# Norms two blocks ahead, output chains in halves, and W_down sums left in PSUM: four edits to a hybrid decoder layer

## The chip, the cores and the metric

The kernel runs on one core of one Trainium2 chip. The metric is device time in microseconds (us). Three runs of the kernel before took 1760.06, 1757.07 and 1756.71 us, with a median of 1757.07. The engines are named as in the profile: PE (matmuls and transposes), PEld (its weight loads), DVE, ACT, POOL, and SP, which issues the DMAs.

## The reference

One decoder layer over 16 learned meta tokens and 1024 tokens, width 1024, all in float32:

```python
def rms_norm(x, g):
    x32 = x.astype(jnp.float32)
    y = x32 * lax.rsqrt(jnp.mean(x32 * x32, axis=-1, keepdims=True) + EPS)
    return (y * g.astype(jnp.float32)).astype(x.dtype)
...
        xn = rms_norm(h, mix_pre_g[l])
        proj = xn @ w_in[l]
...
        y_ssd = ssd_mixer(z, xbc, dt_raw, ssd_conv_w[l], ssd_conv_b[l], ssd_dt_bias[l],
                          ssd_a_log[l], ssd_d[l], ssd_norm_g[l])
        y_sb = rms_norm(stick_breaking_attention(q, k, v).reshape(Bsz, L, SB_WIDTH), sb_norm_g[l])
        mix = jnp.concatenate([y_ssd, y_sb], axis=-1) @ w_out[l]
        h = h + rms_norm(mix, mix_post_g[l])
        xn = rms_norm(h, ffn_pre_g[l])
        gu = xn @ w_up[l]
        g = causal_dwconv(gu[..., :D_FF], ffn_conv_w[l], ffn_conv_b[l])
        f = (jax.nn.gelu(g, approximate=True) * gu[..., D_FF:]) @ w_down[l]
        h = h + rms_norm(f, ffn_post_g[l])
```

`ssd_mixer` is a chunked state-space mixer with a convolution of four taps ahead of it. `stick_breaking_attention` takes, for each of 16 heads of 64, scores z = q.k/8, the logs of sigmoid(z) and of 1 - sigmoid(z), a running sum of the second over the keys behind each key, and the exponential of both together as the weight of v. Keys lie strictly before the query. D_FF is 2816, and the FFN's convolution has three taps.

## The kernel before

**Splits.** Every product is taken at nearly full float32 precision: an operand is split into a high part of the matmul format fp32r (`hi`, a copy on ACT) and a low part (`lo`, original minus high, on DVE or POOL), and three matmuls are summed: hi·hi, lo·hi, hi·lo. A split is thus one ACT copy and one subtraction per tile, and the subtraction's place (DVE or POOL) is chosen line by line.

**Stages in order of time.**

1. *Opening.* The tokens come in nine blocks: block 0 holds the 16 meta rows, blocks 1 to 8 hold 128 tokens each. For each block `load_x` issues the DMA on SP, `square` (L260, ACT) sums the squares, `root` (L190, POOL) makes the reciprocal root, `norm` (L270, DVE, tile xn in a ring of two) scales, and `turn_x` (L282) transposes the block with eight PE matmuls into xtp, copies the high part on ACT (L287) and subtracts the low part on DVE (L289), tile xs. The first projection, pj_dt (L220), reads the first 400 columns, that is blocks 0 to 3. The order on every engine is the order in which this code is written.
2. *SSD part*, then *attention* over eight head pairs p = 0 to 7. In each pair the queries run in eight blocks i. `block_weights` makes scores z (L754) on PE, kp and bt (L755, L756) on ACT, a scan of kp (L762) on DVE and the sum into bt (L764) and a border column cb (L765) on POOL. `block_turn` transposes bt on PE into tw (L776), ACT makes th of it (L778), and `block_mix` multiplies with v into av (L791). A block goes through these stages over three turns of the loop. Between them stand fill steps from the next pair's projections (`fill`, from pj_v and others), so that PE has work while DVE, POOL and ACT are busy. Only PE's order is written by hand here; the others follow the tile framework's priorities. `turn_edge` handles the keys that lie across block borders (edge L419 and L420 on DVE, vtc L422 on PE).
3. *Last pair.* Pair 7 has no next projections. Its fill is the SSD half of the output projection W_out: `ssd_half` makes, for each token block t, two chains mo of 24 matmuls (`out_steps`, L936), one per half of the 1024 output columns, and ACT scales the result into ma (L951). One chain runs per turn of the loop (`run(first, 1)`). The y blocks are split by `split_y` (L925 yh on ACT, L926 yl on POOL). The weights of W_out are woa. `halo_rows` (L905 to L911) multiplies the two y rows ahead of the first token, in four column groups of PE, 64 matmuls of 256 columns (the profile shows two records for each), and takes the result out with four ACT copies mh (L910) and four DMAs into halod. The accumulators mo and halo come from `psum_mm`, a ring of two PSUM banks named mm.
4. *Second half of W_out and the norms* (x2 transposes at L1116), `halo_block` for the two rows ahead of the tokens.
5. *FFN up* in seven Strassen–Winograd products (L1254), with the convolution and the gate (L1319, L1326); their results go to DRAM as fds and fda.
6. *W_down*, also seven products. `DOWN` lists them as (number, left factor, right factor); each has 11 steps, so 77 steps. `down_mm` (L1652) makes 12 matmuls a step, three for each of four row tiles t, into the banks dn. `split_step` (L1568 to L1583) splits both factors of the step three ahead: dh on ACT (L1581), dl on DVE, but on POOL for the right factor in the last 14 steps (`LATE`, L1582). The rings whi and wlo hold three steps. For product 6 it also makes the sum t2 (L1579). `W_SUMS` (L1586) says at which step the sums b11, b21, b12 of weight blocks are made on DVE. When a product is done, `evac2` (L1654 to L1669) adds the bank into up to three accumulators facc in SBUF, one tile per step through the list `todo`. `half_tail`, `close_tail` and `end_tail` (L1682 to L1707) make the last norm: a square on ACT (L1687), a product with the gain on DVE (L1688), the root on POOL (L1697, L1698), the residual on DVE (L1706) and the DMA out. For the upper half of the rows (h = 0) they run beside products 7 and 4, for the lower half at the end, where the last four steps are walked tile by tile.

Tile names carry buffer numbers, which the profile leaves out.

Of the kernel before, what the change touches and what calls it, by code (L numbers as in the profile page):

```python
# [51 lines left out]
def tile_layer(ctx: ExitStack, tc: tile.TileContext, x, meta, rows, parts,  # L52
# [80 lines left out]
    halod = [dr.tile([2, D], F32, name=f"halod{n}", tag=f"halod{n}") for n in range(2)]  # L133
# [92 lines left out]
    with tc.tile_pool(name="pre", bufs=3, side="right") as pre, \  # L226
# [134 lines left out]
    def qkv_steps(p, post):  # L361
# [67 lines left out]
        post += [lambda: turn_v(0), lambda: turn_v(1), turn_edge]  # L429
# [471 lines left out]
    def halo_rows(pool, half, y0, w, acc):  # L901
        for k in range(8):
            for s in range(2):
                for c in range(4):
                    mm(acc[32 * c:32 * c + 2, 0:256], y0[:, k, :], w[k][s][:, 256 * c:256 * c + 256].bitcast(F32),  # L905
                       start=k == 0 and s == 0, stop=k == 7 and s == 1)
        mh = pool.tile([P, 256], F32, tag="ma", name=f"mh{half}", bufs=1)
        for c in range(4):
            rows_ = slice(32 * c, 32 * c + 2)
            nc.scalar.activation(mh[rows_], acc[rows_, 0:256], AF.Copy)  # L910
            nc.sync.dma_start(out=halod[half][:, 256 * c:256 * c + 256], in_=mh[rows_])  # L911
# [7 lines left out]
    def split_y(pool, half, t, tags, yk=None):  # L919
# [6 lines left out]
        nc.gpsimd.tensor_tensor(yl, yk, yh.bitcast(F32), op=ALU.subtract)  # L926
# [15 lines left out]
    def ssd_half(w, ys):  # L942
        for t in range(1, NT + 1):
            y = ys.pop(0)
            if t < NT - 1:
                ys.append(split_y(wp, 0, t + 2, ("whi", "wlo", WB)))

# [6 lines left out]
            yield from out_steps(0, t, w, y, ev)  # L954
# [19 lines left out]
    for p in range(8):  # L974
        for i in range(NT):
# [8 lines left out]
            run(fill, 1 + (i < FILL[p]))  # L984
            run(block)
# [71 lines left out]
    for _ in first:  # L1057
        run(second, 2)
# [659 lines left out]
    for s in range(n2):  # L1718
# [33 lines left out]
        if s + 5 < n2:  # L1752
            fetch_a(s + 4)
# [90 lines left out]
```

## Time and profile before

| | |
|---|---|
| median of three runs | 1757.07 us |
| the profiled execution's own time | 1754.64 us |
| its span | 1752.8 us |
| mean granted PE clock | 0.994 |
| PE busy | 1711.4 us (98%), 11358 matmuls |
| DVE, ACT, POOL busy | 1127.2, 820.2, 890.3 us |
| DMA | 173.87 MB, mean 99 GB/s |

The rows of the profile read as follows. A row of the timeline has start and duration in us, the engine, the line of the kernel, the operation, output and inputs by tile name, the shapes and a count; in brackets stands how long the engine was idle before it and what it was waiting for. A count over one means that the operations of a row follow each other closely. The duration of a matmul is longer than the distance to the next one, because they are pipelined: the distance is what counts. A row of the list of waits has the total time, the number of waits and the longest. A row of the view by stretches has the stretch, its length, busy time and instruction count for each engine, the granted PE clock, the share of DMA time and GB/s. Times are from the start of the span.

### The profile page before, as it was taken

The page shows a single profiled execution, that of the slowest core. Times are in us where ns is not written, and L with a number is a line of the kernel's source. Part 1 is how long each engine was busy: PE and PEld are TensorE (multiplying, and loading weights), DVE is VectorE, ACT ScalarE, POOL GpSimd, SP SyncE. Part 2 cuts the span into 40 slices and gives each one's busy share as a digit, 9 for nine tenths or more (in the row PEclk, how much of TensorE's full clock was granted, in tenths as well). Part 3 has the DMA queues.
Part 4 walks back from the last instruction along what each step waited for, and adds up shares of the span by engine and source line. Part 5 has one row for each costly group of instructions (what it writes and reads, how often), then busy time and mean ns, then how long its engine had stood idle before and what let it go on. Part 6 is the DMA issues. An engine that isn't in the chain of part 4 may idle for free. (4 is left out here: it accounts for less than half of the span.)

```text
span 1752.8 us, 28312 instructions
## 1 busy us (share of the span) xinstructions
PE 1711.4 (98%) x11358; PEld 1505.3 (86%) x11358; DVE 1127.2 (64%) x1225; ACT 820.2 (47%) x1363; POOL 890.3 (51%) x664
## 2 busy tenths in 40 slices
PE   7999999999999999999899989999999999999997
PEld 6999899788999998998678778889998888888885
DVE  5652964875676686668430457676666666757988
ACT  5423653554566566568453344533333333344453
POOL 4323663585566576556451233487776777400015
PEclk9999999999999999999999999999999999999999
DMA  4143343231011110112214543133332222395334
GB/s 161 50 116 93 107 128 105 65 103 38 26 37 37 38 35 27 37 60 74 81 49 145 199 156 132 62 119 98 106 106 91 90 91 90 122 331 185 96 121 162
DMA packets 90655, 173.87 MB, mean 99 GB/s; under 512 B 10694, under 2 KB 35798, under 8 KB 90524
## 3 DMA queue, kind: packets, MB, share of 16 engines
q1 hardware_dynamic: 90524, 172.07, 30.6%
q8 instruction: 89, 1.46, 0.3%
q14 instruction: 42, 0.34, 0.1%
HBM read 122.32 MB, written 49.72 MB: 98 GB/s over the span
## 5 line engine op out<-in xcount | busy, mean ns | idle before, releaser
L764 POOL TENSOR_TENSOR bt<-bt,kp 128x256 f32<-128x256 f32 (+7 forms) x128 | 212.7, 1681 | 180.4 <-DVE kp L762 150.7
L762 DVE TENSOR_TENSOR_SCAN kp<-kp,hold 128x272 f32<-128x272 f32 (+7 forms) x128 | 184.0, 1478 | 26.2 <-ACT kp L755 17.2
L1197 POOL TENSOR_TENSOR wlo<-wr,whi 128x1024 fp32r<-128x1024 f32 x43 | 107.5, 2508 | 38.0 <-ACT whi L1196 38.0
L1652 PE MATMUL dn<-dl,dh 128*128 128x512 f32 x304 | 118.7, 390 | 1.2 <-POOL dl L1582 1.2
L1652 PE MATMUL dn<-dh,dl 128*128 128x512 f32 x304 | 118.6, 390 | 0.1
L1652 PE MATMUL dn<-dh 128*128 128x512 f32 x304 | 118.5, 390 | 0.0
L1697 POOL TENSOR_TENSOR fms<-fms 128x1 f32<-128x1 f32 x8 | 5.6, 694 | 197.9 <-ACT dh L1581 185.8
L755 ACT ACTIVATE kp<-z 128x288 f32<-128x288 f32 (+6 forms) x112 | 82.6, 737 | 47.8 <-PE z L754 22.1
L1581 ACT ACTIVATE dh<-ar 128x512 fp32r<-128x512 f32 x76 | 48.1, 632 | 112.0 <-PE dn L1652 77.4
L1196 ACT ACTIVATE whi<-wr 128x1024 fp32r<-128x1024 f32 x43 | 45.6, 1060 | 114.8 <-PE fX L1254 68.3
L163 PE MATMUL pj_v<-xs,wh_v 128*128 128x400 f32 (+2 forms) x384 | 94.9, 334 | 0.0
L163 PE MATMUL pj_k<-xs,wh_k 128*128 128x400 f32 (+2 forms) x384 | 94.3, 332 | 0.0
L1326 DVE SCALAR_TENSOR_TENSOR ga<-gr,pp,ga 128x1024 f32<-128x1024 f32 x44 | 71.4, 1622 | 34.7 <-ACT ga L1319 33.9
L163 PE MATMUL pj_q<-xs,wh_q 128*128 128x386 f32 (+2 forms) x384 | 93.7, 331 | 0.0
L778 ACT ACTIVATE th<-tw 128x1024 f32<-128x1024 f32 (+2 forms) x96 | 75.7, 818 | 38.0 <-PE tw L776 37.8
L163 PE MATMUL pj_X<-xs,wh_X 128*128 128x400 f32 (+2 forms) x384 | 93.0, 329 | 0.0
L163 PE MATMUL pj_z<-xs,wh_z 128*128 128x386 f32 (+2 forms) x384 | 91.5, 326 | 0.0
L730 DVE CAST qh<-q 128x128 fp32r<-128x128 f32 x64 | 44.1, 690 | 63.9 <-PE z L754 63.6
L776 PE MATMUL tw<-ident,bt 128*128 128x128 f32 x576 | 78.1, 279 | 5.9 <-ACT bt L756 3.0
L1582 DVE TENSOR_TENSOR dl<-ar,dh 128x512 fp32r<-128x512 f32 x76 | 58.4, 768 | 39.1 <-ACT dh L1581 35.9
L756 ACT ACTIVATE bt<-z 128x288 f32<-128x288 f32 (+6 forms) x112 | 82.9, 740 | 0.0
L936 PE MATMUL mo<-woa,yh 128*128 128x512 f32 x256 | 82.4, 396 | 0.0
(556 smaller groups left out, 5532.3 us busy)
## 6 DMA issues: line engine op xcount, KB each, us to landing
wr<-in_w_up SPq DMA_DIRECT2D x44, 512.0 KB, 4.1
fds<-ga SPq DMA_DIRECT2D x44, 256.0 KB, 2.0
b<-in_w_down SPq DMA_DIRECT2D x44, 256.0 KB, 4.7
ar<-fds SPq DMA_DIRECT2D x44, 256.0 KB, 2.6
fda<-ga SPq DMA_DIRECT2D x33, 256.0 KB, 4.5
ar<-fda SPq DMA_DIRECT2D x33, 256.0 KB, 3.0
yk<-yd SPq DMA_DIRECT2D x16, 512.0 KB, 4.5
wor<-in_w_out SPq DMA_DIRECT2D x12, 512.0 KB, 3.9
```

The lines of the kernel that those rows point to most:

```text
L163: mm(acc[:ncol, :n - s], a[:, k, :ncol], xs[c0][:, b, k, s:n], start=(k == 0 and j == 0), stop=(k == KB - 1 and j == 2))
L755: nc.scalar.activation(kp[:, :, a:a + w], z[:, :, :w], AF.Sigmoid, scale=-QSCALE)
L756: nc.scalar.activation(bt[:, :, a:a + w], z[:, :, :w], AF.Sigmoid, scale=QSCALE)
L762: nc.vector.tensor_tensor_scan(kp[:, j][:, ::-1], kp[:, j][:, ::-1], hold[:, L - n:L][:, ::-1], 0.0, op0=ALU.mult, op1=ALU.max)
L764: nc.gpsimd.tensor_tensor(bt[:, j, 0:m], bt[:, j, 0:m], kp[:, j, 1:m + 1], op=ALU.mult)
L776: nc.tensor.transpose(tw[:, j, b, :], bt[:, j, c0:c0 + P], ident)
L778: nc.scalar.activation(th[:, :, :nb, :], tw[:, :, :nb, :], AF.Copy)
L936: mm(acc, u[:, k, :], v[:, cs], start=(k == 0 and j == 0), stop=(k == 7 and j == 2))
L1197: nc.gpsimd.tensor_tensor(l, raw, h.bitcast(F32), op=ALU.subtract)
L1326: nc.vector.scalar_tensor_tensor(v, self.g[jj][:, :, i:i + 256], fconv_w[:, j, i:i + 1], v, op0=ALU.mult, op1=ALU.add)
L1582: (nc.gpsimd.tensor_tensor if k and s >= n2 - LATE else sub)(lo[k], raw, hi[k].bitcast(F32), op=ALU.subtract)
L1652: mm(banks[t], u[0][:, c], v[1], start=(p == 0 and i == 0), stop=(p == NPR - 1 and i == 2))
```

## The change

There are four edits.

**1. Opening.** `load_x(4)` stands ahead of the loads of the dt weights and of B0. Three roots and two norms are issued ahead of the loop; in the loop the norm of block i + 2 is issued ahead of the turn of block i (for i = 3 behind it), and the square and root of block i + 3 behind it.

```diff
         load_x(3)
+        load_x(4)
...
-        for i in range(4, NT + 1):
+        for i in range(5, NT + 1):
...
         for i in range(3):
             square(i)
-        root(0)
-        root(1)
+            root(i)
         norm(0)
+        norm(1)
         for i in range(NT + 1):
+            if i != 3:
+                norm(i + 2)
+            turn_x(i)
             square(i + 3)
-            root(i + 2)
-            norm(i + 1)
-            turn_x(i)
+            root(i + 3)
+            if i == 3:
+                norm(5)
```

DVE from its first norm on, before (xn are norms, xs are low parts):

```order
L270 SCALAR_TENSOR_TENSOR xn_185<-xt_141,rs_pre_177,gpre 16x1024
L270 SCALAR_TENSOR_TENSOR xn_194<-xt_143,rs_pre_181,gpre 128x1024
L289 TENSOR_TENSOR xs_132<-xtp_0_196,xs_132 128x4x16
L289 TENSOR_TENSOR xs_132<-xtp_1_201,xs_132 128x4x16
L270 SCALAR_TENSOR_TENSOR xn_217<-xt_147,rs_pre_190,gpre 128x1024
L289 TENSOR_TENSOR xs_132<-xtp_0_219,xs_132 128x4x128
L289 TENSOR_TENSOR xs_132<-xtp_1_224,xs_132 128x4x128
L270 SCALAR_TENSOR_TENSOR xn_243<-xt_149,rs_pre_213,gpre 128x1024
L289 TENSOR_TENSOR xs_132<-xtp_0_245,xs_132 128x4x128
```

The same place after:

```order
L272 SCALAR_TENSOR_TENSOR xn_191<-xt_143,rs_pre_173,gpre 16x1024
L272 SCALAR_TENSOR_TENSOR xn_193<-xt_145,rs_pre_180,gpre 128x1024
L272 SCALAR_TENSOR_TENSOR xn_195<-xt_149,rs_pre_187,gpre 128x1024
L291 TENSOR_TENSOR xs_134<-xtp_0_197,xs_134 128x4x16
L291 TENSOR_TENSOR xs_134<-xtp_1_202,xs_134 128x4x16
L272 SCALAR_TENSOR_TENSOR xn_218<-xt_151,rs_pre_214,gpre 128x1024
L291 TENSOR_TENSOR xs_134<-xtp_0_220,xs_134 128x4x128
L291 TENSOR_TENSOR xs_134<-xtp_1_225,xs_134 128x4x128
L272 SCALAR_TENSOR_TENSOR xn_244<-xt_153,rs_pre_237,gpre 128x1024
```

Each norm moved up by one place in the row of low parts.

**2. Last pair.** `out_steps` yields after the fourth of eight k steps too, so a chain comes in two halves of 12 matmuls; one half is issued before the rest of a block's scores, one behind it. The low parts of the first two y blocks go to DVE, the second is split after the first half chain, later ones after the first chain of their turn. `turn_edge` stands two fill steps later in pair 7.

```diff
-        post += [lambda: turn_v(0), lambda: turn_v(1), turn_edge]
+        post += [lambda: turn_v(0), lambda: turn_v(1)] + [lambda: None] * (2 * (p == 7)) + [turn_edge]
...
-    def split_y(pool, half, t, tags, yk=None):
+    def split_y(pool, half, t, tags, yk=None, eng=nc.gpsimd):
...
-        nc.gpsimd.tensor_tensor(yl, yk, yh.bitcast(F32), op=ALU.subtract)
+        eng.tensor_tensor(yl, yk, yh.bitcast(F32), op=ALU.subtract)
...
             for k, (wh, wl) in enumerate(w):
+                if k == 4:
+                    yield
...
             run(fill, 1 + (i < FILL[p]))
+            if first:
+                run(first, 1)
             run(block)
...
-            while len(ys1) < min(2, left[1]):
-                ys1.append(split_y(wp, 0, len(ys1) + 1, ("whi", "wlo", WB), yk[len(ys1)]))
+            if left[1] and not ys1:
+                ys1.append(split_y(wp, 0, 1, ("whi", "wlo", WB), yk[0], nc.vector))
...
                 run(first, 1)
+                ys1.append(split_y(wp, 0, 2, ("whi", "wlo", WB), yk[1], nc.vector))
```

The two other loops that run these chains take two halves at a time where they took one chain, and the loop that runs the preparation of the second half's weights takes one step per half chain where it took two per chain.

PE where block 7 of pair 6 is turned, before (tw_7 are its transposes, mo_1_0 is the first chain):

```order
L791 MATMUL av_6_8926<-th_6_1_8893,v_8157 64x128 x6
L422 MATMUL vtc_8945<-ident,edge_8942 128x128
L776 MATMUL tw_7_0_8952<-ident,bt_7_8730 128x128 x8
L776 MATMUL tw_7_1_8963<-ident,bt_7_8730 128x128 x8
L936 MATMUL mo_1_0_8985<-woa_8393,yh_1_8721 128x512
```

After, with the rows behind the first half chain:

```order
L759 MATMUL z_2_0_8986<-kl_8218,qh_2_8915 128x400 x2
L796 MATMUL av_7_9004<-th_7_0_8949,v_8159 64x128 x8
L796 MATMUL av_7_9004<-th_7_1_8960,v_8159 64x128 x8
L427 MATMUL vtc_9025<-ident,edge_9022 128x128
L944 MATMUL mo_1_0_8967<-woa_8638,yh_1_8723 128x512
L944 MATMUL mo_1_0_8967<-woa_8638,yl_1_8724 128x512
```

The transposes tw_7 now follow av_6 directly, and vtc stands behind av_7, between the two halves of the first chain.

**3. Halo.** `halo_rows` uses matmuls of 512 columns: the high part of the weights goes to column groups 0 and 1, the low part to 2 and 3. That makes 32 matmuls. The result is taken out in two passes of four ACT copies and four DMAs, both through one buffer mh. `halod` has four parts instead of two, and `halo_block` loads four and adds them with two more DVE operations.

```diff
-            for s in range(2):
-                for c in range(4):
-                    mm(acc[32 * c:32 * c + 2, 0:256], y0[:, k, :], w[k][s][:, 256 * c:256 * c + 256].bitcast(F32),
-                       start=k == 0 and s == 0, stop=k == 7 and s == 1)
...
+            for c in range(4):
+                mm(acc[32 * c:32 * c + 2, :], y0[:, k, :], w[k][c // 2][:, 512 * (c % 2):512 * (c % 2) + 512].bitcast(F32),
+                   start=k == 0, stop=k == 7)
+        for a in (0, 256):
+            mh = pool.tile([P, 256], F32, tag="ma", name=f"mh{half}_{a}", bufs=1)
```

ACT behind the first halo, before (ma is the evacuation of a chain, th and sqb belong to the attention):

```order
L951 ACTIVATE ma_8984<-mo_1_1_9055,r_ssd 128x512
L925 ACTIVATE yh_4_9213<-yk_4_9211 128x1024
L910 ACTIVATE mh_9147<-halo_9082 2x256 x4
L755 ACTIVATE kp_3_9162<-z_3_0_9164 128x2x264
L756 ACTIVATE bt_3_9163<-z_3_0_9164 128x2x264
L755 ACTIVATE kp_3_9162<-z_3_1_9173 128x2x264
L756 ACTIVATE bt_3_9163<-z_3_1_9173 128x2x264
L794 ACTIVATE ysc_9194<-av_0_9191 128x128
L821 ACTIVATE sqb_9201<-ysc_8434 128x1024
L778 ACTIVATE th_1_0_9209<-tw_1_0_9204 128x2x256
```

After:

```order
L916 ACTIVATE mh_0_9103<-halo_9070 2x256 x4
L760 ACTIVATE kp_3_9127<-z_3_0_9129 128x2x264
L761 ACTIVATE bt_3_9128<-z_3_0_9129 128x2x264
L760 ACTIVATE kp_3_9127<-z_3_1_9138 128x2x264
L761 ACTIVATE bt_3_9128<-z_3_1_9138 128x2x264
L799 ACTIVATE ysc_9159<-av_0_9156 128x128
L826 ACTIVATE sqb_9166<-ysc_8436 128x1024
L916 ACTIVATE mh_256_9112<-halo_9070 2x256 x4
L956 ACTIVATE ma_8966<-mo_1_1_9057,r_ssd 128x512
L783 ACTIVATE th_1_0_9188<-tw_1_0_9183 128x2x256
```

The evacuation of mo_1_1 moved from ahead of the halo's copies to behind the second set of them.

**4. W_down.** The products run in the order 1, 2, 6, 5, 3, 7, 4. Sums of products that the algorithm needs stay in PSUM: each row tile has two banks, A and B; product 6 accumulates onto 1, product 3 onto 5, and 7 and 4 onto 1 + 6. Where the next product writes the same bank, `evac2` runs directly behind the last step (product 5 by four ACT copies, product 7 by four DVE adds); products 1, 2, 6 and 3 are still taken out through `todo`. The accumulator facc[1, 0] is gone, and the last `half_tail` reads the bank. All low parts are made on DVE, the last three steps instead of four are walked tile by tile, and the last step has no buffers of its own any more. The b11 sums stand at steps 18 to 28, one per step, where they stood at every second step from 15 on.

```diff
-DOWN = [(1, "a11", "b11"), (2, "a12", "b21"), (3, "s4", "b22"), (6, "s2", "t2"), (5, "s1", "b11"), (7, "s3", "b12"),
+DOWN = [(1, "a11", "b11"), (2, "a12", "b21"), (6, "s2", "t2"), (5, "s1", "b11"), (3, "s4", "b22"), (7, "s3", "b12"),
         (4, "a22", "b21")]
+BANK = {1: "A", 2: "B", 6: "A", 5: "B", 3: "B", 7: "A", 4: "A"}
...
-            (nc.gpsimd.tensor_tensor if k and s >= n2 - LATE else sub)(lo[k], raw, hi[k].bitcast(F32), op=ALU.subtract)
+            sub(lo[:, k], raw, hi[:, k].bitcast(F32), op=ALU.subtract)
...
-        for at, args in ((15 + 2 * k, ("b11", "b12", "b11", ALU.subtract)), (16 + 2 * k, ("b21", "b21", "b22", ALU.subtract)),
+        for at, args in ((18 + k, ("b11", "b12", "b11", ALU.subtract)), (16 + 2 * k, ("b21", "b21", "b22", ALU.subtract)),
...
+        dst = facc[{1: (0, 0), 2: (0, 0), 6: (0, 1), 5: (1, 1), 3: (0, 1), 7: (1, 1)}[n] + (t,)]
+        if n in (1, 6, 5):
+            nc.scalar.activation(dst, acc, AF.Copy)
+        else:
+            add(dst, acc, dst, op=ALU.add)
...
-        f = facc[h, hf, t]
+        f = banks["A", t] if (h, hf) == (1, 0) else facc[h, hf, t]
...
-        if s > 2 and s < n2 - 4:
+        if s > 2 and s < n2 - 3:
             down_mm(s, (3, 0, 1, 2))
-        elif s == n2 - 4:
+            if p == NPR - 1 and n in (5, 7):
+                for t in (3, 0, 1, 2):
+                    evac2(n, t, banks[BANK[n], t])
+        elif s == n2 - 3:
```

DVE in the first steps of product 6, before (t are the sums t2, b the sums of weights, dl the low parts):

```order
L1579 TENSOR_TENSOR t_4_15839<-b_4_15429,b_4_14910 128x512
L1582 TENSOR_TENSOR dl_15838<-ar_15811,dh_15837 128x512
L1582 TENSOR_TENSOR dl_15838<-t_4_15839,dh_15837 128x512
L1586 TENSOR_TENSOR b_9_15259<-b_9_15259,b_9_15580 128x512
L1579 TENSOR_TENSOR t_5_15863<-b_5_15454,b_5_14912 128x512
L1582 TENSOR_TENSOR dl_15862<-ar_15835,dh_15861 128x512
L1582 TENSOR_TENSOR dl_15862<-t_5_15863,dh_15861 128x512
```

The same steps after:

```order
L1585 TENSOR_TENSOR t_4_15547<-b_4_15384,b_4_14870 128x512
L1588 TENSOR_TENSOR dl_15546<-ar_15514,dh_15545 128x512
L1588 TENSOR_TENSOR dl_15546<-t_4_15547,dh_15545 128x512
L1592 TENSOR_TENSOR b_5_14872<-b_5_15432,b_5_14872 128x512
L1667 TENSOR_TENSOR facc_15087<-dnB_15229,facc_15087 128x512
L1585 TENSOR_TENSOR t_5_15573<-b_5_15408,b_5_14872 128x512
L1588 TENSOR_TENSOR dl_15572<-ar_15543,dh_15571 128x512
L1588 TENSOR_TENSOR dl_15572<-t_5_15573,dh_15571 128x512
L1592 TENSOR_TENSOR b_4_15145<-b_4_15145,b_4_15384 128x512
L1592 TENSOR_TENSOR b_6_14874<-b_6_15459,b_6_14874 128x512
L1667 TENSOR_TENSOR facc_15088<-dnB_15233,facc_15088 128x512
```

A step had four operations there and has five or six now, with a weight sum or two and an evacuation between the low parts. Where product 4 follows product 7, DVE has this after:

```order
L1588 TENSOR_TENSOR dl_16473<-ar_16439,dh_16472 128x512
L1588 TENSOR_TENSOR dl_16473<-b_1_15057,dh_16472 128x512
L1704 SCALAR_TENSOR_TENSOR slott4h<-slott4h,fms_16448 128x1024
L1667 TENSOR_TENSOR facc_15098<-dnA_14947,facc_15098 128x512
L1667 TENSOR_TENSOR facc_15095<-dnA_14957,facc_15095 128x512
L1667 TENSOR_TENSOR facc_15096<-dnA_14961,facc_15096 128x512
L1667 TENSOR_TENSOR facc_15097<-dnA_14965,facc_15097 128x512
L1588 TENSOR_TENSOR dl_16499<-ar_16470,dh_16498 128x512
L1588 TENSOR_TENSOR dl_16499<-b_2_15101,dh_16498 128x512
```

The end of a tail (slott4h) and two low parts stand ahead of the four adds that empty the banks.

More of the change, by code (lines that the diff above doesn't have):

```diff
@@ L952, in ev @@
                 nc.sync.dma_start(out=mixd[t - 1][:, cs], in_=ma[:, cs])
-            yield from out_steps(0, t, w, y, ev)
+            for i, _ in enumerate(out_steps(0, t, w, y, ev)):
+                if i == 1 and t < NT - 1:
+                    ys.append(split_y(wp, 0, t + 2, ("whi", "wlo", WB)))
+                yield
     wo1 = ExitStack()
@@ L1026, in tile_layer @@
             run(begin_turn())
-        run(first, 1)
+        run(first, 2)
     edge = edge_turn(7)
-    run(first, 1)
+    run(first, 2)
     edge_mix(7, edge)
@@ L1057, in tile_layer @@
     for _ in first:
-        run(second, 2)
+        run(second, 1)
     run(second)
@@ L1422, in tile_layer @@
         steps = out_steps(1, t, wres2, ys.pop(0), ev2)
-        run(steps, 1)
+        run(steps, 2)
         run(norm, 1)
@@ L1725, in tile_layer @@
             for t in range(4):
-                for k in range(4):
+                for k in range(3):
                     down_mm(s + k, (t,))
-                evac2(n, t, banks[t])
                 half_tail(1, t, 0)
```

78 lines of the change are left out of this document (26 added, 52 removed).

## Prediction

> **What bounds the kernel.** I read the page's first part, then the busy time of each engine by stretches (us, busy and instruction count of PE, PEld, DVE, ACT, POOL, then granted clock, DMA share, GB/s), then the list of PE's waits.
>
> ```profile
> PE 1711.4 (98%) x11358; PEld 1505.3 (86%) x11358; DVE 1127.2 (64%) x1225; ACT 820.2 (47%) x1363; POOL 890.3 (51%) x664
> ...
> 0.00:50.00 50.00, 37.85 (x227) 33.90 (x228) 25.31 (x37) 24.94 (x46) 18.00 (x35) 1.00 0.40 142
> ...
> 800.00:850.00 50.00, 45.08 (x383) 38.60 (x383) 40.66 (x35) 35.11 (x55) 35.38 (x23) 0.93 0.22 66
> 850.00:900.00 50.00, 47.77 (x402) 35.86 (x397) 17.32 (x23) 23.50 (x42) 23.10 (x21) 0.97 0.17 59
> 900.00:950.00 50.00, 48.47 (x320) 39.24 (x319) 6.51 (x6) 17.94 (x26) 18.46 (x10) 1.00 0.21 70
> ...
> PE xtp L282 <- DVE xn L270: 12.2, 5, 8.3
> ```
>
> PE is the bound: 1711.4 of 1752.8 us, so all idle time together is 41.4 us. No edit takes matmuls of full size away, so the change can only earn part of that idle time and of slow-clock time. It sits where the change works: 12.2 us before 50 us (opening), 8.7 us from 800 to 950 (last head pair), and the end of W_down. The rest lies in stages that the diff leaves in their order; in the stage after the last pair its halves of chains run in pairs, which is the old order.
>
> **Opening.** The rows are PE's turns, then DVE's norms, then ACT's square of block 4.
>
> ```profile
> 12.42 1.97 PE L282 MATMUL xtp<-ident,xn 128*128 128x128 f32 x8 [0.96 <-DVE xn L270]
> 16.66 1.94 PE L282 MATMUL xtp<-ident,xn 128*128 128x128 f32 x8 [2.27 <-DVE xn L270]
> 19.05 1.61 PE L282 MATMUL xtp<-ident,xn 128*128 128x128 f32 x8 [0.45 <-DVE xn L270]
> 20.41 3.14 PE L220 MATMUL pj_dt<-xs,wh_dt 128*32 128x400 f32 x16
> ...
> 6.97 2.47 DVE L270 SCALAR_TENSOR_TENSOR xn<-xt,rs_pre,gpre 16x1024 f32<-16x1024 f32 x2 [4.49 <-DMA gpre<-in_rows]
> ...
> 19.20 1.29 DVE L289 TENSOR_TENSOR xs<-xtp,xs 128x512 fp32r<-128x512 f32 x2 [0.29 <-ACT xs L287]
> ...
> 12.37 1.06 ACT L260 ACTIVATE junk<-xt 128x1024 f32<-128x1024 f32 x1 [1.46 <-DMA xt<-in_x]
> ```
>
> After its first two norms (2.47 us, to 9.44) DVE alternates norm and low part, and PE waits 0.96 + 2.27 + 0.45 = 3.68 us; from pj_dt on it is fed. After the change DVE still does three norms of about 1.24, the meta rows' small low part (some 0.3) and three of 1.29 before pj_dt: 7.9 us, so 17.4 if it never waits. It does wait: the xn ring keeps two buffers, so the norm of block 4 needs the turn of block 2 (1.97 us from about 11.6, right behind norm 2, so 13.5) and block 4's square and root. I put that norm at 14.4; with 1.24 + 1.29 + 1.29 and a drain of 0.4 the last low part is out at about 18.65. Moving the load of block 4 ahead on SP ends ACT's 1.46 us wait, and what is moved behind it (raw_dt, the B0 weights) comes one load later. Gain 20.41 - 18.65 = **1.75 us**; ends: 3.0 (no waits) and a loss of 0.5 (weights late, for ACT holds their splits between the others). I take the value between, since ring and squares still pace DVE.
>
> **Last pair, up to the turn of block 7.** PE, POOL, DVE; then the same block of pair 5, where no out-projection runs; then the clock.
>
> ```profile
> 835.87 0.37 PE L422 MATMUL vtc<-ident,edge 128*128 128x128 f32 x1 [2.01 <-DVE edge L420]
> ...
> 837.70 1.11 PE L776 MATMUL tw<-ident,bt 128*128 128x128 f32 x4 [0.60 <-POOL bt L764]
> 840.05 1.97 PE L776 MATMUL tw<-ident,bt 128*128 128x128 f32 x8 [1.24 <-ACT bt L756]
> ...
> 827.34 4.38 POOL L926 TENSOR_TENSOR yl<-yk,yh 128x1024 fp32r<-128x1024 f32 x1
> 831.69 5.96 POOL L764 TENSOR_TENSOR bt<-bt,kp 128x1024 f32<-128x1024 f32 x2
> 837.61 1.22 POOL L765 TENSOR_TENSOR cb<-bt,kp 128x30 f32<-128x30 f32 x1
> ...
> 827.20 6.70 DVE L762 TENSOR_TENSOR_SCAN kp<-kp,hold 128x1040 f32<-128x1040 f32 x2
> ...
> 700.99 4.53 DVE L762 TENSOR_TENSOR_SCAN kp<-kp,hold 128x1040 f32<-128x1040 f32 x2
> ...
> 703.45 5.82 POOL L764 TENSOR_TENSOR bt<-bt,kp 128x1024 f32<-128x1024 f32 x2 [2.79 <-DVE kp L762]
> 709.23 0.24 POOL L765 TENSOR_TENSOR cb<-bt,kp 128x30 f32<-128x30 f32 x1
> ...
> 835.00:840.00 5.00, 2.34 (x9) 1.57 (x9) 4.97 (x5) 1.14 (x2) 3.83 (x3) 0.60 0.08 12
> 840.00:845.00 5.00, 4.95 (x20) 4.37 (x21) 3.16 (x7) 2.80 (x5) 3.28 (x7) 0.72 0.64 202
> ```
>
> The second half of the turn starts 1.22 us after POOL's cb ends (838.83), since ACT's next kp/bt stand behind cb and free the bank. In pair 5 the same bt end 709.27 - 700.99 = 8.28 us after the scan starts; here 10.45, with yl between. If yl_2 simply leaves POOL, bt end at 835.5, cb (0.24, as there) at 835.7: gain 3.1. But yl_2 goes onto DVE ahead of the scans (its wait for ACT's yh_2 is over by then; that one keeps its place on ACT), where about 1.25 us, as a norm of that size, may push the scans by 0.8, and cb may again take its 1.22: cb then ends at 837.5, gain 1.3. I take the middle, **2.2 us**; the vtc wait goes with it, because vtc now stands behind av of block 7.
>
> The Trainium skill (SBUF — State Buffer, section "SBUF: two separate sides") says that a GpSimd operation and a DVE operation with two SBUF inputs lock each other out whole. The trace agrees (scans of 4.53 take 6.70 beside yl, yl takes 4.38); by that rule the low part still costs POOL its time on DVE, and the term would be 1.3.
>
> **Last pair, the rest.** PE's waits from 845 to 950, and for the new order ACT's rows behind the halo:
>
> ```profile
> PE tw L776 <- ACT bt L756: 1.3, 2, 1.0
> PE tw L776 <- issue: 1.3, 2, 0.8
> PE z L754 <- ACT bt L756: 0.6, 1, 0.6
> PE tw L776 <- POOL yl L926: 0.6, 1, 0.6
> ...
> 856.33 7.09 PE L905 MATMUL halo<-woa,y 128*2 128x256 f32 x128
> 866.30 0.63 PE L776 MATMUL tw<-ident,bt 128*128 128x128 f32 x4 [0.78 <-issue]
> ...
> 863.49 1.58 ACT L910 ACTIVATE mh<-halo 2x256 f32<-2x256 f32 x4 [5.41 <-PE halo L905]
> 867.23 1.09 ACT L821 ACTIVATE sqb<-ysc 128x1024 f32<-128x1024 f32 x1
> ```
>
> That is 3.8 us of waits for a chain DVE-POOL-ACT. Half a chain (12 matmuls, 2.72 us, below) now stands before each, longer than any; the last one or two come when the steps run short. I take **2.8**, ends 1 and 3.8. Against it stands a new wait. The accumulators have two banks: the chain of block 1's second half, the halo and the next chain now follow so that mo_2_0 needs the evacuation of mo_1_1, whose second half has just run. ACT does ahead of it, from the halo's end: mh, kp/bt and sqb as before (863.49 to 868.32, 4.8 us), four more mh copies (1.58) and the evacuation itself (0.7, as an add of that size below), 7.1 us. PE has 2.1 us (863.42 to 865.52) + 2.72 + 0.4 = 5.2. So PE waits **2.0 us**, ends 0.8 and 3.7 (the second mh uses the first's buffer and so waits for its DMAs; behind it on ACT stand that evacuation and the next block's th).
>
> The halo has half the matmuls at twice the columns: 7.09/128 = 55 ns each, and I take time as following columns: 0, ends -3.5 (if issue sets it) and +0.3. Its eight extra DMAs of 2 KB rows go on SP, where no one waits; two extra DVE operations lie where PE waits for POOL's root. Sum for the last pair -2.2 - 2.8 + 2.0 = **-3.0**.
>
> **W_down.** PE's dn matmuls (the first row from the stretch up to 1700 us), a stretch inside, the end:
>
> ```profile
> L1652 PE MATMUL dn<-dh x249: 389/389/395, 1531.2 to 1699.8; 128*128 128x512 f32 x125
> ...
> L1652 PE MATMUL dn<-d,d x12: 389/390/505, 1734.9 to 1744.6; 128*128 128x512 f32 x12
> ...
> 1650.00:1680.00 30.00, 30.00 (x134) 24.86 (x133) 28.17 (x47) 12.70 (x22) 0.00 (x0) 1.00 0.33 97
> ...
> 1712.60 2.33 DVE L1706 SCALAR_TENSOR_TENSOR slott4h<-slott4h,fms 128x1024 f32<-128x1024 f32 x1 [0.72 <-POOL fms L1698]
> ...
> 1734.52 0.51 PE L1652 MATMUL dn<-dl,dh 128*128 128x512 f32 x1 [0.64 <-POOL dl L1582]
> ...
> 1745.03 0.69 DVE L1663 TENSOR_TENSOR facc<-dn,facc 128x512 f32<-128x512 f32 x1 [0.16 <-PE dn L1652]
> ```
>
> 168.6 us for 248 triples is 0.680 each, 2.72 a step of four. 924 matmuls at 0.2267 would put the last start at 1531.2 + 209.2 = 1740.4; it is at 1744.6. So 4.2 us go in the last 14 steps, where POOL makes low parts late and stretches DVE (2.33 for one of a norm's kind and size, which took 1.24). With all low parts on DVE that goes: **-4.2**. At the end the add (0.69) leaves the path, as the last tail reads PSUM: **-0.7**.
>
> New there: (1) DVE. Up to product 6 its program has 40 operations in 8 steps. 47 in 30 us, PE unwaiting, gives at most 0.60 each: 24.1 us against 8 x 2.72 = 21.8, 2.3 behind. Low parts run up to two steps ahead: 5.4 us, less some 2 for the copies and low parts themselves, leaves 3.4. So 0 if the lead is whole, 2.3 if none is left; I take 1.0. (2) From product 7 to 4 the bank must be emptied before PE goes on, and on DVE two low parts and an end of a tail (0.6 for the copy, 1.2, 1.3, and the evacuation's 0.7: 3.8 against 2.72) stand first: 1.1, ends 0 and 2.5. Behind that stand the low parts of two steps later. (3) The last split without its own buffers: 0.4. From 5 to 3 ACT copies, and has half its time free (12.70 of 30): 0. The weights that are now wanted in another order come from a DMA that is a third busy there (0.33): 0. W_down: -4.9 + 2.5 = **-2.4**.
>
> **Sum.** -1.75 - 3.0 - 2.4 = -7.2 us: 1754.64 gives 1747.4. The profiled execution is 2.43 us under the median of the three runs, so on that median 1757.07 - 7.2 = about 1750.
>
> **Rivals.**
> - *Every new wait is covered.* The 2.0, 1.0, 1.1 and 0.4 fall away: 1745.4. For it: ACT and DVE have idle time around these places. Against: the orders are fixed and queues do not overtake.
> - *The last pair gains nothing.* The wait moves from yl to the scans and banks, and a longer new wait brings the slow clock: the stretch after the 2.01 us wait ran at 0.72, 1.4 us of 5. Then 0 instead of -3.0: 1753. The Trainium skill (TensorE: Matmul & The Clock Gate, Part 1) has the clock fall only after about 3.4 us idle; by that rule a 2 us wait is free of it. The trace differs here: 0.60 with no single wait over 2.01.
> - *Slower: DVE becomes W_down's bound.* The page's group of low parts:
>
> ```profile
> L1582 DVE TENSOR_TENSOR dl<-ar,dh 128x512 fp32r<-128x512 f32 x76 | 58.4, 768 | 39.1 <-ACT dh L1581 35.9
> ```
>
> If its operations take the page's mean, 768 ns, 40 take 30.7 us against 21.8: 8.9 late, less 3.4 ahead, 5.5; four steps of 4.5 before and some 14 of 4 after add 2.9 and 4.9. W_down then goes to -4.9 + 1.5 + 13.3 = +9.9, all to +5.2: 1762. It decides from about 0.72 us an operation, where these terms reach 8 and eat all gains. Against: that mean comes from the stretch where POOL works too; inside it is 0.60.
>
> **How the numbers follow.** Forecast 0.52 (own range 1746.5 to 1753.5), all covered 0.13, last pair without gain 0.20, DVE bound 0.15. The range 1744 to 1757 takes in the first three with their ends. 0.2% (3.5 us, about what a measurement of this kernel tells from no change) sets the bound at 1753.6: faster 0.49 + 0.13 + 0.11 = 0.73, same 0.13, slower 0.14.
>
> **What the profile would show.** Right: pj_dt near 18.7 us; no vtc wait, the second tw of block 7 about 2 us earlier than opening's shift explains; one PE wait of about 2 us at mo_2_0 on ACT's ma; in W_down no POOL low parts, small waits around the sixth to tenth step of product 6 and where 4 begins. Wrong: dn waits for DVE dl over many steps, or a clock under 0.8 around mo_2_0.

## The result and the profile after

The changed kernel takes 1752.21 us (median of six runs, 1749.49 to 1753.36), against 1759.91 us for six runs of the kernel before on the same chips. The ratio is 0.9962, with a 95% interval of 0.9953 to 0.9972: 6.7 us less (4.9 to 8.3); the two medians lie 7.7 us apart. The forecast was 7.2 us less. That is close, but the parts of the sum are not what was predicted, as the experiments show.

The profiled execution of the changed kernel took 1753.36 us, the slowest of its six, and that of the kernel before (1754.64 us) is faster than all six of its runs (1756.71 to 1760.09), so the two profiles lie only 1.3 us apart. Some stretches of the changed kernel and its list of waits:

```profile
0.00:50.00 50.00, 39.85 (x249) 35.97 (x250) 24.90 (x37) 25.90 (x47) 22.22 (x36) 1.00 0.40 142
...
800.00:850.00 50.00, 45.88 (x394) 39.23 (x393) 40.23 (x38) 35.75 (x57) 31.43 (x24) 0.97 0.22 65
850.00:900.00 50.00, 49.13 (x343) 34.86 (x343) 18.26 (x21) 24.73 (x45) 24.76 (x20) 0.97 0.18 59
...
PE xtp L284 <- DVE xn L272: 9.5, 4, 8.4
PE x2tp L1127 <- DVE oxn L1121: 6.6, 2, 6.3
...
PE dnA L1658 <- DVE facc L1667: 1.8, 1, 1.8
```

The kernel before had, for the FFN's norms:

```profile
PE x2tp L1116 <- DVE oxn L1110: 5.1, 2, 4.8
```

PE's wait for the opening's norms fell from 12.2 to 9.5 us, and PE's busy time in the first 50 us rose by 2.0. In the last pair, from 800 to 900 us, busy time rose by 0.8 + 1.4. Three things are new or larger: the wait for x2tp (5.1, now 6.6 us; the norms between the output projection and the FFN), the wait for facc in W_down (1.8 us), and one that has no row of its own, DVE's backlog in product 6, shown below.

Opening, from PE's timeline:

```profile
17.20 0.43 PE L221 MATMUL pj_dt<-xs,wh_dt 128*32 128x400 f32 x1
18.14 2.92 PE L221 MATMUL pj_dt<-xs,wh_dt 128*32 128x400 f32 x15 [0.52 <-DVE xs L291]
20.90 1.03 PE L284 MATMUL xtp<-ident,xn 128*128 128x128 f32 x8
```

All but the first of pj_dt's matmuls now run from 18.14 us (before 20.41), and the next turn starts at 20.90, where it stood at 23.50: 2.6 us earlier.

Last pair, PE, POOL and DVE:

```profile
835.40 0.66 PE L781 MATMUL tw<-ident,bt 128*128 128x128 f32 x4 [1.21 <-POOL bt L769]
837.76 1.83 PE L781 MATMUL tw<-ident,bt 128*128 128x128 f32 x8 [1.70 <-ACT bt L761]
...
865.21 0.50 PE L944 MATMUL mo<-woa,yh 128*128 128x512 f32 x1 [0.87 <-ACT mh L916]
906.91 0.66 PE L781 MATMUL tw<-ident,bt 128*128 128x128 f32 x4 [1.30 <-ACT bt L761]
...
820.68 6.06 POOL L769 TENSOR_TENSOR bt<-bt,kp 128x896 f32<-128x896 f32 x2 [3.68 <-DVE kp L767]
...
835.32 1.22 POOL L770 TENSOR_TENSOR cb<-bt,kp 128x30 f32<-128x30 f32 x1
...
822.37 2.73 DVE L932 TENSOR_TENSOR yl<-yk,yh 128x1024 fp32r<-128x1024 f32 x1
827.07 4.53 DVE L767 TENSOR_TENSOR_SCAN kp<-kp,hold 128x1040 f32<-128x1040 f32 x2
```

The scans of block 7 take 4.53 us again (6.70 before), and cb ends 9.47 us after they start (11.63 before). The wait for the edge is gone, the predicted wait at mo_2_0 is there with 0.87 us, and of the waits behind it one of 1.30 is left. But yl took 2.73 us on DVE, and bt of block 6 took 6.06 (5.11 before).

W_down, one form of PE's matmuls and a stretch, then DVE in product 6 and at the switch to product 4:

```profile
L1658 PE MATMUL dnA<-dl,dh x176: 387/390/505, 1530.2 to 1743.3; 128*128 128x512 f32 x176
...
1590.00:1620.00 30.00, 29.96 (x126) 22.85 (x126) 28.99 (x48) 12.51 (x22) 0.00 (x0) 1.00 0.38 104
...
1604.16 0.68 DVE L1585 TENSOR_TENSOR t<-b,b 128x512 f32<-128x512 f32 x1
1604.76 0.68 DVE L1588 TENSOR_TENSOR dl<-ar,dh 128x512 fp32r<-128x512 f32 x1
1605.54 0.69 DVE L1588 TENSOR_TENSOR dl<-t,dh 128x512 fp32r<-128x512 f32 x1
1606.15 0.69 DVE L1592 TENSOR_TENSOR b<-b,b 128x512 f32<-128x512 f32 x1
1606.75 0.68 DVE L1667 TENSOR_TENSOR facc<-dnB,facc 128x512 f32<-128x512 f32 x1
1607.35 0.68 DVE L1585 TENSOR_TENSOR t<-b,b 128x512 f32<-128x512 f32 x1
...
1710.89 1.28 DVE L1704 SCALAR_TENSOR_TENSOR slott4h<-slott4h,fms 128x1024 f32<-128x1024 f32 x1 [0.44 <-POOL fms L1696]
1712.09 2.48 DVE L1667 TENSOR_TENSOR facc<-dnA,facc 128x512 f32<-128x512 f32 x4
...
1712.92 0.47 PE L1658 MATMUL dnA<-dh 128*128 128x512 f32 x1 [1.75 <-DVE facc L1667]
```

The low parts no longer wait for POOL anywhere in W_down. Yet from the start of the first dn matmul (1529.8 us) to that of the last (1743.3) it takes 213.5 us, where it took 213.4 (1531.2 to 1744.6). Between 1590 and 1620 us PE has 126 matmuls where an undisturbed stretch of 30 us has 134: 8 fewer at 0.224 us, 1.8 us. DVE is busy for 28.99 of the 30 us. A step with five DVE operations takes 1607.35 - 1604.16 = 3.19 us there, against PE's 2.72. The second stall is plain in the last rows: the end of a tail stands ahead of the four adds that empty the banks, and PE waits 1.75 us.

### The profile page after: what moved, and what is told of

It is laid out like the page before. It is cut to its first block, busy times and chain, and to the rows that moved or that the text cites. A ratio compares the mean times of both kernels' runs of the same rounds, so it can differ in the third digit from the quotient of the medians.

```text
span 1751.3 us, 28046 instructions
## 1 busy us (share of the span) xinstructions
PE 1712.6 (98%) x11230; PEld 1502.4 (86%) x11230; DVE 1119.2 (64%) x1223; ACT 825.1 (47%) x1375; POOL 863.6 (49%) x648
## 5 line engine op out<-in xcount | busy, mean ns | idle before, releaser
L1588 DVE TENSOR_TENSOR dl<-ar,dh 128x512 fp32r<-128x512 f32 x77 | 53.2, 691 | 51.0 <-ACT dh L1587 51.0
L796 PE MATMUL av<-th,v 128*64 128x128 f32 x1152 | 78.3, 281 | 0.0
L781 PEld LDWEIGHTS tw<-ident,bt 128*128 128x128 f32 x576 | 65.9, 142 | 10.4 <-ACT bt L761 4.2
L796 PEld LDWEIGHTS av<-th,v 128*64 128x64 f32 x1152 | 62.3, 138 | 13.9 <-issue 11.3
```

What stands on the lines that cost most here:

```text
L781: nc.tensor.transpose(tw[:, j, b, :], bt[:, j, c0:c0 + P], ident)
L796: mm(av[halves[j], :], v[:, kb, halves[j]], th[:, j, b, :], start=kb == 0, stop=kb == i)
```

## The experiments

All ratios are to the kernel before on the same chip, with 95% intervals; us are worked out on 1758 us. First each part of the change alone.

**Opening alone.** The two edits of the opening on the kernel before:

```diff
         load_x(3)
+        load_x(4)
...
+            if i != 3:
+                norm(i + 2)
+            turn_x(i)
             square(i + 3)
```

> The kernel before with the opening's part alone. The profile of the changed kernel has pj_dt 2.3 us earlier and the second pass at the end of the state-space stage 3.3 us earlier. If that is the opening's own worth, this kernel is 2.5 to 3.5 us faster than before, with the lead of pj_dt again 2 to 2.5 us. If the lead is lost again up to the attention (in that profile it fell to 0.4 us beside two stretches at clock 0.83), it is 0 to 1 us faster, and the same stretches run slow again.

Ratio 0.9979 (0.997 to 0.9987): 3.7 us less (2.3 to 5.3). The longest wait for x2tp is 4.8 us, as before, and pj_dt runs from 18.07. In the profile of this kernel the two stretches of which the expectation speaks have full clock, and the lead stays (the first matmul of pj_q starts 2.7 us earlier, the last 2.6):

```profile
320.00:330.00 10.00, 9.12 (x64) 6.71 (x64) 5.24 (x12) 8.66 (x22) 4.97 (x3) 1.00 0.01 2
420.00:430.00 10.00, 9.96 (x81) 8.76 (x82) 7.19 (x10) 6.59 (x13) 5.95 (x5) 1.00 0.00 0
```

In the changed kernel's profile they read:

```profile
320.00:330.00 10.00, 9.62 (x60) 7.78 (x61) 3.75 (x9) 7.95 (x22) 4.09 (x3) 0.83 0.01 2
420.00:430.00 10.00, 9.96 (x71) 8.54 (x71) 4.05 (x9) 5.26 (x10) 5.75 (x6) 0.83 0.02 7
```

A mean of 0.83 over 10 us is 3.4 us at half clock. Of the fourteen profiles of this document four have such a piece from 320 to 330 us and six from 420 to 430, with and without the opening's edits, so the loss of the lead in that profile is no effect of the change.

**Load of block 4 first, alone.** Of the opening only

```diff
         load_x(3)
+        load_x(4)
```

> The kernel before with the load of block 4 ahead of the weights, and the norms where they were. If ACT's wait for that load was what held the third turn, 1 to 1.5 us of the opening's gain come already here and pj_dt starts at about 19 us. If the order of the norms on DVE is what counts, pj_dt stays at 20 to 20.7 us and the time is that of before within 1 us.

Ratio 0.9999 (0.999 to 1.0007): nothing. PE's three waits together shrink (0.89 + 0.77 + 0.80 us, before 3.68) and pj_dt starts sooner, but it then takes longer and the next turn comes no earlier than before (23.93 against 23.50):

```profile
19.57 4.52 PE L220 MATMUL pj_dt<-xs,wh_dt 128*32 128x400 f32 x16
23.93 1.03 PE L283 MATMUL xtp<-ident,xn 128*128 128x128 f32 x8
```

The gain needs the norms ahead. Whether they would bring it without this load was not run.

**Last pair alone.** Chains in halves, low parts on DVE, edge turn later; the old halo:

```diff
+            if first:
+                run(first, 1)
             run(block)
...
+                ys1.append(split_y(wp, 0, 2, ("whi", "wlo", WB), yk[1], nc.vector))
```

> The last pair's part alone (chains in halves, two low parts on DVE, the later edge turn), with the old halo. As predicted -3.0 us. Without the second pass of halo copies the new wait for the accumulator's evacuation should be short (the copies of 1.58 us are missing ahead of it), so -3 to -4 us. If the chain through POOL still paces the pair, -1 to 0.

Ratio 0.9972 (0.996 to 0.9984): 4.9 us less (2.8 to 7.0). Around the turn of block 7 the waits are those of the whole change, but the clock stays full, where the kernel before showed 0.60 and 0.72:

```profile
837.27 0.66 PE L776 MATMUL tw<-ident,bt 128*128 128x128 f32 x4 [1.30 <-POOL bt L764]
839.62 1.09 PE L776 MATMUL tw<-ident,bt 128*128 128x128 f32 x8 [1.69 <-ACT bt L756]
...
835.00:840.00 5.00, 2.01 (x19) 1.35 (x16) 4.97 (x6) 1.14 (x2) 3.40 (x3) 1.00 0.12 23
840.00:845.00 5.00, 4.31 (x27) 3.18 (x27) 2.73 (x7) 3.01 (x4) 3.71 (x7) 1.00 0.59 192
```

Without the halo's second set of copies there is no wait at mo_2_0. So the wait of 0.87 us belongs to the halo's part. What this run has left behind the turn is a wait of 0.69 for ACT's th (at 844.18) and one of 1.30 (at 906.82).

**Last pair with the low parts on POOL.** As above, with

```diff
-                ys1.append(split_y(wp, 0, 2, ("whi", "wlo", WB), yk[1], nc.vector))
+                ys1.append(split_y(wp, 0, 2, ("whi", "wlo", WB), yk[1], nc.gpsimd))
```

and the same for the first y block.

> The last pair's part alone, but with the first two low parts back on POOL (only the halves, the later split and the later edge turn are left). If the two low parts on DVE are what shortens the way to the turn of block 7 (the prediction's 2.2 us), the turn's second half starts again as late as before and 1.5 to 3 us of the 4.9 us are lost: 2 to 3.5 us faster than before. If the locking of DVE and POOL makes it the same on either engine, it is as fast as the part with the low parts on DVE, within 1 us of -4.9.

Ratio 0.9979 (0.997 to 0.9987): 3.7 us less. The turn's second half starts at 842.89 us, and the clock falls as it did before:

```profile
842.89 1.97 PE L776 MATMUL tw<-ident,bt 128*128 128x128 f32 x8 [1.69 <-ACT bt L756]
...
830.00:850.00 20.00, 15.07 (x116) 12.11 (x114) 15.96 (x15) 9.79 (x16) 16.70 (x12) 0.83 0.18 54
```

POOL's bt of the blocks ahead ran 2.9 us later in this execution than before, and 1.5 us later in the one with the low parts on DVE (839.62). So the low parts on DVE bring 842.89 - 839.62 - 1.4 = 1.9 us at this place. In time the two differ by 1.2 us, which the intervals do not separate.

**Halo alone.**

```diff
-                for c in range(4):
-                    mm(acc[32 * c:32 * c + 2, 0:256], y0[:, k, :], w[k][s][:, 256 * c:256 * c + 256].bitcast(F32),
...
+            for c in range(4):
+                mm(acc[32 * c:32 * c + 2, :], y0[:, k, :], w[k][c // 2][:, 512 * (c % 2):512 * (c % 2) + 512].bitcast(F32),
```

> The halo's part alone. Predicted 0. If PE's time follows the columns, 7.1 us per halo stay. If it follows the number of matmuls, two times 3.5 us go. If the two extra DVE operations and the extra DMAs delay the norms between the output projection and the FFN (in the changed kernel's profile PE waited 6.3 there instead of 4.8 us), it is 1 to 1.5 us slower.

Ratio 1.0011 (1.0002 to 1.0019): 1.9 us more. PE's time for the halo is that of the columns (7.05 against 7.09 us), and the wait behind the output projection grew:

```profile
861.10 7.05 PE L904 MATMUL halo<-woa,y 128*2 128x512 f32 x64
...
PE x2tp L1117 <- DVE oxn L1111: 6.6, 2, 6.3
...
1003.48 1.28 DVE L1101 SCALAR_TENSOR_TENSOR mb<-mb,rs_mo,gpost 128x1024 f32<-128x1024 f32 x1 [3.85 <-POOL rs_mo L190]
1004.68 1.26 DVE L1176 SCALAR_TENSOR_TENSOR mb<-mo,r_sb,mb 2x1024 f32<-2x1024 f32 x1
1005.88 1.21 DVE L1102 TENSOR_TENSOR mb<-mb,xr 128x1024 f32<-128x1024 f32 x1
```

The same steps before:

```profile
999.24 1.29 DVE L1100 SCALAR_TENSOR_TENSOR mb<-mb,rs_mo,gpost 128x1024 f32<-128x1024 f32 x1 [3.85 <-POOL rs_mo L190]
1000.57 1.23 DVE L1101 TENSOR_TENSOR mb<-mb,xr 128x1024 f32<-128x1024 f32 x1
```

One of the extra operations (L1176) stands between the two steps of the norm that PE waits for. They start 2.40 us apart, before 1.33; this 1.07 us is most of the longer wait (6.3 against 4.8).

**W_down alone.** The order of the products, the banks and the rest of that part:

```diff
+BANK = {1: "A", 2: "B", 6: "A", 5: "B", 3: "B", 7: "A", 4: "A"}
...
+            sub(lo[:, k], raw, hi[:, k].bitcast(F32), op=ALU.subtract)
```

> The part on W_down alone. Predicted -2.4 us. The profile of the changed kernel has a wait of 1.75 us where product 4 begins and 8 matmuls too few (1.8 us) in product 6, together as much as the 4.2 us lost before; by it only the tail's 0.7 us remain, so -0.2 to -1 us.

Ratio 1.0005 (0.9996 to 1.0014): 0.9 us more (-0.7 to 2.5), so no gain is seen. From first to last dn matmul it takes 213.5 us (1533.5 to 1747.0), with the same wait of 1.8 us.

**All low parts on DVE, nothing else.**

```diff
-    n2, LATE = len(steps2), 14
+    n2, LATE = len(steps2), 0
```

> The kernel before with all low parts of W_down on DVE (the 14 late ones moved from POOL), and nothing else. The prediction's first term says that POOL's low parts cost 4.2 us there: then 3 to 4.2 us faster, and no wait for POOL in the last 14 steps. The rival: DVE is as full there without POOL's ring of late steps, and the waits move to DVE: within 1 us of before.

Ratio 0.998 (0.997 to 0.999): 3.5 us less (1.8 to 5.3). From first to last dn matmul it takes 210.4 us instead of 213.4, and no wait is left there:

```profile
L1652 PE MATMUL dn<-dh x304: 389/389/499, 1533.9 to 1743.2; 128*128 128x512 f32 x152
L1652 PE MATMUL dn<-d,d x12: 389/392/502, 1735.0 to 1744.3; 128*128 128x512 f32 x12
```

So the part on W_down contains one edit that earns 3 us, and others that take it away again.

**Weight sums later.** On the changed kernel:

```diff
-                         (16 + 2 * k, ("b21", "b21", "b22", ALU.subtract)),
+                         (30 + k, ("b21", "b21", "b22", ALU.subtract)),
```

> The changed kernel with the b21 sums at steps 30 to 40 instead of every second step from 16 on, so that the steps of product 6 have four or five DVE operations instead of five or six. If the 8 missing matmuls between 1590 and 1620 us are DVE's backlog, 134 per 30 us come back there and W_down is 1.5 to 1.9 us shorter (213.5 to about 211.7 us from the first to the last dn matmul). If ACT's copies or the DMAs set it, nothing changes.

Ratio 0.9946 (0.9931 to 0.9961), which the intervals do not quite separate from the changed kernel's 0.9962. In the trace W_down takes 211.8 us, 1.7 less, and the stretch in product 6 is whole again, while the wait of 1.8 us for facc stays:

```profile
1588.00:1618.00 30.00, 30.00 (x134) 24.86 (x133) 27.16 (x44) 13.25 (x24) 0.00 (x0) 1.00 0.36 98
```

**A free place at the switch to product 4.** On the changed kernel:

```diff
-                    todo += [whole, lambda t=t: end_tail(0, t)]
+                    todo += [whole] + [lambda: None] * (t == 2) + [lambda t=t: end_tail(0, t)]
```

> The changed kernel with one empty place in the list of late work, so that no end of a tail stands ahead of the four adds where product 4 begins. If that operation holds the bank, the wait of 1.75 us at product 4's first matmul goes and W_down is 1.5 to 1.9 us shorter. If the two low parts alone make the adds late, about 0.5 us of it stay.

Ratio 0.9951 (0.9936 to 0.9966), again not separated from the changed kernel's in time. W_down takes 211.8 us, again 1.7 less. The adds start at 1709.85 with no tail ahead of them, and no wait for facc is left; the shortage in product 6 stays (126 matmuls from 1590 to 1620 us):

```profile
1709.25 0.68 DVE L1588 TENSOR_TENSOR dl<-b,dh 128x512 fp32r<-128x512 f32 x1
1709.85 2.48 DVE L1667 TENSOR_TENSOR facc<-dnA,facc 128x512 f32<-128x512 f32 x4
```

**Both mends, without the halo's part.** Opening, last pair and W_down with the two edits above; `halo_rows` and `halo_block` as before.

> Opening, last pair and W_down with both mends, and the old halo. If the parts add: -3.7 (opening), -4.9 (last pair), +0.9 (W_down) and -3.5 (mends) give 11 us less than before, some 5 us less than the changed kernel, of which 1.5 to 2 us come from the halo's part. PE's wait between the output projection and the FFN is then about 5.6 us, not 6.3. If the mends or the halo do not matter, it equals the changed kernel.

Ratio 0.9938 (0.9924 to 0.9953): 10.9 us less (8.3 to 13.4), as added up. W_down takes 210.1 us, and the longest wait before the FFN is 5.4 us:

```profile
PE x2tp L1126 <- DVE oxn L1120: 5.8, 2, 5.4
```

The last two runs were on one chip: the opening and the last pair with nothing but `LATE = 0` in W_down, and the version just told once more.

> Opening, last pair and all low parts of W_down on DVE, with the old order of the products, the old evacuations and the old halo. If the parts add: -3.7 - 4.9 - 3.5 = 12 us less than before, as fast as the version with the sums left in PSUM and both mends (within 1 us; that one has the tail's 0.7 us more). Then the sums in PSUM by themselves earn nothing beyond the tail. If leaving the sums in PSUM is worth something, it is 2 us or more slower than that version.

> The version with opening, last pair, W_down with both mends and the old halo once more, on the same chip as the kernel with the old products, so that the two can be compared: 10.9 us under the kernel before as in its first run (interval 8.3 to 13.4), and within 1 us of the other if the sums in PSUM earn only the tail's 0.7 us.

The first has a ratio of 0.9931 (0.9917 to 0.9944), the second 0.9927 (0.9915 to 0.994): 12.1 and 12.8 us less, which the intervals do not tell apart. From first to last dn matmul they take 210.4 and 210.1 us. So no gain of the sums left in PSUM is seen beyond the shorter tail. Both versions beat the changed kernel, and the first needs only one number changed in W_down.

## Why the prediction came out right, and where its steps did not

| part | forecast, us | measured alone, us |
|---|---|---|
| opening | -1.75 | -3.7 |
| last pair and halo | -3.0 | -4.9 and +1.9 |
| W_down | -2.4 | +0.9 |
| sum | -7.2 | -5.8 |

The whole measured -6.7; within the intervals, the parts add up. That the forecast was met is luck: gains that were taken too small offset losses that were taken too small. Even the last pair and the halo, together -3.0 as forecast, come to that from other terms.

**Opening: right, too small.** The step gave 1.75 us, the part alone measured 3.7 (2.3 to 5.3). The low parts that gate pj_dt let it run on at 18.14 us, predicted 18.65. What the step left out is that one matmul of pj_dt runs ahead of that (17.20), so that the turn behind it stands 2.6 us earlier. Its end "no waits" (3.0) was nearer than the value between. What is left of the 3.7 us is not located; the interval takes in 2.6. The load on SP, in which the step saw ACT's 1.46 us, earned nothing by itself.

**Last pair: right in mechanism, three terms off.** The way to the turn of block 7 was to shorten by 2.2 us; the runs with and without the low parts on DVE differ by 1.9 there. The lower end, reckoned with yl pushing the scans, was 1.3. The Trainium skill (SBUF — State Buffer, section "SBUF: two separate sides") says that a DVE operation with two SBUF inputs and a GpSimd operation that reads SBUF lock each other out. The trace agrees again: yl takes 2.73 us on DVE beside POOL's bt of block 6, and 1.25 where POOL is idle. The term of 1.3 that the prediction drew from that rule was too small all the same, because yl now stands beside bt of block 6 and no longer between the scans and bt of block 7. The later waits were to give 2.8 of 3.8: in the run without the halo's change one of 1.30 and one of 0.69 are left, so about 1.8 net. The wait at mo_2_0 was to cost 2.0 and cost 0.87.

What the sum had no term for is the slow clock. Of the fourteen profiles, seven have the first two low parts on POOL: the kernel before, the five parts of the change run alone that leave them there (opening, load, halo, W_down, its low parts) and the run that puts them back. In all seven the mean clock from 830 to 850 us is 0.83, 3.4 us of missing clock, and the waits in the turn of block 7 add to 3.85 to 4.8 us. In the seven with the low parts on DVE these waits add to 3.0 or less and the clock is 1.00 or 0.91; two of those at 1.00 have 0.93 from 805 to 830 instead. So the shorter way also brings back clock. PE waits during part of that time, so this is worth less than 3.4 us: in the kernel before half clock lasts from the last wait of the turn (840.05) to about 842.8, which by estimate costs 1.4 us. The prediction priced such a stretch at just that, but only as a loss in a rival.

**Halo: the step that failed in sign.** It gave 0 and measured +1.9 (0.4 to 3.3). PE's time was right to 0.04 us. The failing sentence is that the two extra DVE operations "lie where PE waits for POOL's root". One does lie there in the halo's own run, but DVE itself is in that chain, one step further on, and the operation that comes first there delays the norm by 1.07 us. In the changed kernel the extra operations stand elsewhere, and one of them runs beside a low part on POOL:

```profile
992.57 1.26 DVE L1186 SCALAR_TENSOR_TENSOR mb<-mo,r_sb,mb 2x1024 f32<-2x1024 f32 x1
...
993.10 3.00 POOL L932 TENSOR_TENSOR yl<-yk,yh 128x1024 fp32r<-128x1024 f32 x1 [10.09 <-ACT yh L931]
```

This low part stands ahead of the root on POOL. In the run of the last pair alone, where the DVE operation is over by then, it takes 2.39 us, and the root comes 0.6 us sooner. That the one operation lengthens the other is likely, as with yl above, but no run tests it. Nor is all of the changed kernel's longer wait the halo's: the longest wait for x2tp is 4.8 us before, 5.4 to 5.6 in the four runs with the last pair's part and the old halo, 4.9 with that part but the low parts on POOL, and 6.1 to 6.3 in the three runs with both parts. How the last pair's part lengthens it, no run shows.

**W_down: the step that failed in size.** It gave -2.4 and measured +0.9 (-0.7 to 2.5); in the profile of the changed kernel PE's time grew by 0.1 us and the tail shrank by 0.7. Both sides of the sum were mis-sized. The gain was sound but smaller: low parts on DVE alone gave 3.0 us in PE's time and 3.5 in all, where 4.2 was predicted; 1.2 us over the ideal 209.2 stay when POOL has no low part left, and no run shows what they are. The tail's 0.7 was right (from PE's end to the end of DVE's last operation 4.77 us before and 4.03 after). The new stalls were put at 2.5 and came to 3.4 (213.5 us against 210.1 with both mends). Of these the backlog of product 6 was 1.7, predicted 1.0 of at most 2.3; PE first runs short at its eighth step (1608.75 us), as was forecast. 0.60 us an operation was right, but in each step DVE also waits for ACT's copy of the sum that it has just made (0.78 instead of 0.60 between two operations); the low parts are ready only 2.8 us ahead of PE when product 6 begins (1586.8 against 1589.6), where 3.4 was taken; and four steps of six and five operations in turn take 14.0 us against PE's 10.9. The bank switch was 1.7, predicted 1.1, since the tail's end there waited 0.44 for POOL's root too. The last term, 0.4 for the last split, is not seen: with both mends PE's time is no longer than in the old order (210.1 and 210.4).

**Rivals.** DVE as the bound of W_down, the slower rival, had the right place and too high a price: DVE's operations stayed at 0.60 us, and the backlog was 1.7, not 13. That all new waits would be covered was wrong, and that the last pair would gain nothing was wrong. The second of these let the clock fall behind a wait of 2 us, and shorter waits do it too: waits of 1.21 and 1.70 us in the changed kernel stood beside a clock of 0.79 and 0.86, and nearly the same waits in the part alone beside 1.00. The rule of the Trainium skill (TensorE: Matmul & The Clock Gate, Part 1) that was set against it, a fall after an idle window of about 3.4 us, does not hold strictly in this trace.

## What to carry to other kernels

Operations that are added to an engine that seems idle have to be placed in its queue: if the engine waits for something that ends in work for the bound engine, what stands first can delay that work by most of its length (1.07 of 1.26 us here), and beside POOL it may lengthen what POOL does (0.6 us, likely but not tested). Count an engine's operations per step of the bound engine over the fullest run of steps, and add the hand-overs to another engine inside the step; here a lead of one step (2.8 us) did not outlast four steps that were together 3.1 us too long. And take a change of many edits apart before keeping it: here one number gave as much as the whole mended rework of the last stage.

## What was not expected of the hardware

The clock falls in pieces of about 3.4 us at half speed. The two in the changed kernel's profile, and what PE does ahead of the second:

```profile
322.50:326.00 3.50, 3.50 (x17) 3.40 (x16) 1.46 (x4) 2.06 (x8) 1.62 (x1) 0.51 0.00 0
421.50:425.00 3.50, 3.50 (x22) 2.94 (x20) 1.67 (x4) 2.29 (x5) 1.82 (x1) 0.51 0.00 0
...
419.21 2.07 PE L444 MATMUL pta<-ones,sq 128*2 128x1 f32 x18
```

They cost nearly the whole lead that this profile had: 3.3 us at the first matmul of pj_q, 0.4 at the last. The first comes 2 us behind a wait of 0.88 us. The second comes behind no wait at all, but behind 18 matmuls of one column, in which PE counts as busy. The opening's own profile has the same wait of 0.88 us (at 321.00) and full clock, so at these two places the fall differs from execution to execution of the same work; at the turn of block 7 it came in all seven profiles whose waits there add to 3.85 us or more. The runs of one kernel spread by 4 to 6 us (1749.49 to 1753.36 after, 1754.1 to 1760.21 for 28 runs of the kernel before), so single profiles compare stages well only between places where the clock reads the same.
